# A decoder step on one Trainium2 core: split keys stored and loaded again, cached memory steps spread, sample projections on two banks

## The chip, the cores and the metric

The kernel runs on one core of a Trainium2 chip. The core has five engines with instruction streams of their own: TensorE (PE in the profile, its weight loads PEld), VectorE (DVE), ScalarE (ACT), GpSimd (POOL) and SyncE (SP, used here only to issue DMAs). Engines meet through semaphores; DMA queues are fed by SP, POOL and ACT. Operands stay in the on-chip state buffer, products go to PSUM, which has eight banks of 512 fp32 columns by 128 partitions.

The metric is the device time of one execution in microseconds. The kernel before was run three times: 1905.01, 1898.7 and 1908.0 us, median 1905.01.

## What is computed

One step of a hybrid decoder layer, for a prompt group of 1024 tokens and a sample group of 8 sequences with one token each, which share the weights (model width 1024). In the reference, cut to what matters:

```
q, k, v, logf, u, z = mixer_inputs(rmsnorm(xp, g_mix), w_in, b_f, g_sgu_v)     # prompt: 8 heads of 64
xp = xp + merge_heads(fox_prompt(q, k, v, logf), sgu_prompt(...), ..., w_o)
xp = xp + cross_attend(rmsnorm(xp, g_cross), mk, mv, w_cq, w_co)               # 256 memory rows, 4 heads of 256
xp = xp + conv_ffn(rmsnorm(xp, g_ffn), ...)                                    # 2816 gated columns

s = einsum(q, k) * 64 ** -0.5 + (cq - ck);  s[kpos > qpos] = -inf              # causal, with forget sums
o = einsum(softmax(s), v)

xs = ... the same for the sample: 8192 cached tokens through a page table,
     cross_attend with the cached keys and values of 256 memory rows per sequence
```

Everything is fp32 to the tolerance of the reference. TensorE multiplies at reduced precision per pass, so the kernel writes an operand as a high part and a remainder (`h` = rounded copy, `l` = x - h) and adds three products.

## The kernel before, in words

**Two generators.** `prompt()` yields the main work with a cost per yield. The sample's work is a second generator; the driver adds each main cost to an account and, while the account holds at least `PACE[phase]`, advances the sample by one step and subtracts it (L1793-1799). In the sample's last phase, `rest`, one step costs 2.9. Program text in that order goes through a scheduler that simulates the engines and sets the order of the instructions on each of them; `behind(e)` (L1269) makes what follows wait in that order for the latest main instruction of engine `e`.

**The prompt** goes in two halves of 512 rows: projections, attention, output projection, cross attention, feed-forward. Attention of half `hf` is `attention(hf)` (L674). It runs over four head pairs, two heads of 64 in the rows 0-63 and 64-127. For a pair:

- `load(hp)` brings q, k and v rows by three DMAs on SP (k and v of all 512 or 1024 keys).
- `setup(hp, ...)`: q rows are transposed on PE (L700) and split (L706, L707 on ACT, L720 on DVE), the forget sums come by POOL DMAs from `cq_d` and `ck_d` (L708, L717). Then, for each half `kh` of the keys, four transposes on PE (L725), a copy of each head to the high part on ACT (L729), a cast that repeats it in the rows 64-127 on POOL (L731), and the remainder by a subtraction on DVE (L736). In the first half there is one key half, in the second half two. The second half's setup of the next pair is started within the present pair.
- `scores` (L751-755): for each query block of 128 a product with the high keys and one with the low keys, per 512 columns, and the mask. In the second half a score has 640 to 1024 columns and fills a double bank; then a maximum on DVE (L760) and the exponential on ACT (L761), which frees the bank.
- `turn` transposes the exponentials (L779), ACT or DVE copy them (L786, L784), `values` multiplies them with v (L795, L804 copies the result), `back` transposes and scales (L815, L817).

**PSUM.** In the second half `BA()` and `BA2()` share two double banks in turn. A pair of `BA()` calls gets the two halves of one double bank; a score takes a whole one. Scores, q transposes and key transposes follow each other on these two.

**Buffers.** `U` is a ring of 18 buffers of 4 KB per partition, `T2` of 7 of 2 KB, `KV` of 4 of 8 KB.

**The sample** first reads its 8192 cached tokens in gathers on POOL (L1326 keys, L1385 values), multiplies and reduces keys on DVE (L1332, L1336), and multiplies values on PE (L1391). Then comes `sample_rest` (L1499): `sample_proj` for w_o and w_cq (each in two column halves, `sample_out` evacuates one), the query rows through DRAM (`q2s_d`), and the cached memory steps, eight of them, one per sequence: two broadcast loads of query rows and one load of 256 memory keys on POOL, two multiplies (L1555) and one reduce (L1556) on DVE, then a yield. Softmax, the cached memory values, w_co (L1634 and after) and the sample's feed-forward follow.

**The prompt's feed-forward** runs beside these: three products per tile (L269-271), weights split by L232 (ACT) and L233 (DVE), the convolution of a tile on DVE (L1214, L1215, L1217, L1221), which reads the PSUM bank and so frees it.

Of the kernel before, what the change touches and what calls it, by code (L numbers as in the profile page):

```python
# [18 lines left out]
P = 128  # L19
# [10 lines left out]
FF = 2816  # L30
NF = FF // P
NPAGE = 64
EPS = 1e-6
NEG = -1e30
UW = 1024
# [43 lines left out]
def build(nc, tc, ctx, a, phases=None):  # L79
# [31 lines left out]
    def U(shape, dt=F32):  # L111
        n = 1
        for s in shape[1:]:
            n *= s
        t = upool.tile([P, UW], dt, tag="u", bufs=NU, name=nm("u"))[:, :n]
        if len(shape) == 3:
            t = t.rearrange("p (a b) -> p a b", b=shape[2])
        return t
# [87 lines left out]
    sgn_d = dram.tile([T, AW], F32, tag="sgn_d", name="sgn_d")  # L206
    cq_d = dram.tile([NH, 4, T], F32, tag="cq_d", name="cq_d")
    ck_d = dram.tile([NH, 4, T], F32, tag="ck_d", name="ck_d")
    an_d = dram.tile([T, AW], F32, tag="an_d", name="an_d")
    qs_d = dram.tile([NB, AW], F32, tag="qs_d", name="qs_d")  # L210
    us_d = dram.tile([NB, AW], F32, tag="us_d", name="us_d")
# [468 lines left out]
    def attention(hf, late=None, at=3):  # L680
# [3 lines left out]
        def load(hp):  # L684
            cs = slice(hp * P, (hp + 1) * P)
            qn = T2().rearrange("p (i c) -> p i c", c=P)
            nc.sync.dma_start(qn, q_d[hf * 512 : (hf + 1) * 512, cs].rearrange("(i p) c -> p i c", p=P))
            if hf == 0:
                kvn = U([P, 2 * nk, P])
                kn, vn = kvn[:, :nk, :], kvn[:, nk:, :]  # L690
            else:
                kn, vn = U([P, nk, P]), U([P, nk, P])
            nc.sync.dma_start(kn, k_d[: nk * P, cs].rearrange("(i p) c -> p i c", p=P))
            nc.sync.dma_start(vn, v_d[: nk * P, cs].rearrange("(i p) c -> p i c", p=P))
            return qn, kn, vn

        def setup(hp, qn, kn, vn):
            tr = (MS, BB, BA)[SB]()
            for i in range(4):
                nc.tensor.transpose(tr[:, i * P : (i + 1) * P], qn[:, i, :], ident)  # L700
            qab, ka, kb = [], [], []
            for j in range(2):
                h = hp * 2 + j
                rows = slice(64 * j, 64 * j + 64)
                qq = U([P, 2, 512], F32R)
                nc.scalar.activation(qq[0:64, 0, :], tr[rows, :], AF.Copy)  # L706
                nc.scalar.activation(qq[0:64, 1, :], tr[rows, :], AF.Copy)  # L707
                nc.gpsimd.dma_start(qq[64:68, 1, :], cq_d[h, :, hf * 512 : (hf + 1) * 512])  # L708
                qab.append(qq)
                if hf == 0:  # L710
                    kab = U([P, 2, 512], F32R)
                    ka.append(kab[:, 0, :])
                    kb.append(kab[:, 1, :])
                else:
                    ka.append(U([P, nk * P], F32R))
                    kb.append(U([P, nk * P], F32R))
                nc.gpsimd.dma_start(kb[j][64:68, :], ck_d[h, :, : nk * P])  # L717
            for j, qq in enumerate(qab):
                rows = slice(64 * j, 64 * j + 64)
                nc.vector.tensor_tensor(qq[64:128, 0, :], tr[rows, :], qq[0:64, 0, :].bitcast(F32), op=ALU.subtract)  # L720
            for kh in range(hf + 1):
                yield
                tr = (MS, BB, BA)[SB]()
                for i in range(4):
                    nc.tensor.transpose(tr[:, i * P : (i + 1) * P], kn[:, kh * 4 + i, :], ident)  # L725
                s = slice(kh * 512, kh * 512 + 512)
                for j in range(2):
                    rows = slice(64 * j, 64 * j + 64)
                    nc.scalar.activation(ka[j][0:64, s], tr[rows, :], AF.Copy)  # L729
                    if KP & 1 << hf:  # L730
                        nc.gpsimd.tensor_copy(ka[j][64:128, s], ka[j][0:64, s].bitcast(F32))  # L731
                    else:
                        nc.scalar.activation(ka[j][64:128, s], tr[rows, :], AF.Copy)
                for j in range(2):
                    rows = slice(64 * j, 64 * j + 64)
                    nc.vector.tensor_tensor(kb[j][0:64, s], tr[rows, :], ka[j][0:64, s].bitcast(F32), op=ALU.subtract)  # L736
            got.append((qab, ka, kb, vn))

        def scores(qkv, ls, blk, j, ii):
# [740 lines left out]
    def sample_out(n, ps, fin):  # L1480
        t = D2()
        nc.scalar.activation(t, ps, AF.Copy)
        yield 1
        ps2 = MS()
        mmul(ps2[:8, :], selS, t, start=True, stop=True)
        fin(n, ps2[:8, :])

    def sample_proj(w, xT, fin):
        for n in range(2):
            ps = MS()  # L1490
            for kk in range(4):
                if kk % 2 == 0:
                    raw = KV().rearrange("p (k n) -> p k n", n=512)
                    nc.gpsimd.dma_start(raw, w[kk * 256 : (kk + 2) * 256, n * 512 : (n + 1) * 512].rearrange("(k p) n -> p k n", p=P))
                    yield 1
                sample_mm(ps, raw[:, (kk % 2) * 2 : (kk % 2) * 2 + 2, :], kk, xT, 512)
            yield from sample_out(n, ps, fin)

    def sample_rest(xs):  # L1499
        yield 1  # L1500
# [45 lines left out]
        for b in range(8):  # L1546
            qb = [D2(), D2()]
            for n in range(2):
                nc.gpsimd.dma_start(qb[n], q2s_d[b : b + 1, n * 512 : (n + 1) * 512].broadcast_to((P, 512)))
            kv = KV()  # L1550
            nc.gpsimd.dma_start(kv.rearrange("p (a c) -> p a c", c=D), a["cmk"][b].rearrange("(a p) c -> p a c", p=P))
            kvv = kv.rearrange("p (a c) -> p a c", c=D)
            for n in range(2):
                kn = kvv[:, :, n * 512 : (n + 1) * 512]
                nc.vector.tensor_tensor(kn, kn, qb[n].unsqueeze(1).broadcast_to((P, 2, 512)), op=ALU.mult)  # L1555
            nc.vector.tensor_reduce(sS[:, :, b, :], kv.rearrange("p (a h d) -> p a h d", a=2, h=4), axis=AX.X, op=ALU.add)  # L1556
            yield 1
        yield 1
        tr = MS()
        for mt in range(2):  # L1560
# [225 lines left out]
    for t in prompt():  # L1786
        ins = nc.cur_bb.bb.instructions
        for e in (ENG.DVE, ENG.PE):
            for i in range(len(ins) - 1, max(seen, len(ins) - 400) - 1, -1):
                if ins[i].engine == e:  # L1790
                    last[e] = ins[i]
                    break
        acc[0] += t  # L1793
        most = int(t / PACE[phase[1] or phase[0]]) + 1
        while bgs and not held[0] and most and acc[0] >= PACE[phase[1] or phase[0]]:
            most -= 1
            acc[0] -= PACE[phase[1] or phase[0]]
            if next(bgs[0], None) is None:
                bgs.pop()
        seen = len(nc.cur_bb.bb.instructions)  # L1800
    for _ in bgs.pop() if bgs else ():
        pass
# [90 lines left out]
```

## Time and profile before

| | |
|---|---|
| three runs | 1905.01, 1898.7, 1908.0 us |
| the profiled execution | 1899.86 us |
| its span | 1898.1 us |
| mean granted clock of PE | 0.979 |
| PE busy | 1817.0 us, 96% |
| DVE, ACT, POOL busy | 1394.5, 755.7, 490.6 us |
| first half's attention | about 240 to 340 us of the span |
| second half's attention | about 375 to 510 us |
| the sample's cached memory steps on DVE | about 1572 to 1632 us |

How to read the rows. A row of the timeline has the start in us, the duration, the engine, the line, the operation, out<-in by the program's names with the shape, and in brackets the idle time of the engine before it with what ended it. "xN" stands for N instructions in one row. A row of the waits says which engine and line waited for which, the total in us, how often, and the longest. A row of windows has the stretch, its length, the busy time of PE, PEld, DVE, ACT and POOL, the granted clock of PE, the DMA share and GB/s. Matmuls are pipelined: a duration includes a part in which the next is already running, so the pace is read from the distance of two starts.

### The profile page before, as it was taken

What the parts mean: (1) busy time and instruction counts of PE and PEld (TensorE: products, weight loads), DVE (VectorE), ACT (ScalarE), POOL (GpSimd) and SP (SyncE); (2) the same over time, 40 slices, a digit from 0 to 9 for tenths busy, and PEclk for the clock granted to TensorE, in tenths of its full rate; (3) what the DMA queues carried; (4) which work ended last, traced back from release to release, by engine and by line L of the source; (5) the groups of instructions that cost most, each with busy time, mean ns of one, the idle gap of its engine ahead of it and who ended that gap; (6) DMA issues with size and microseconds to landing.
All of it is one profiled execution on the core that took longest, in us unless ns stands there. A gap on an engine that the chain in (4) does not pass through costs nothing.

```text
span 1898.1 us, 24082 instructions
## 1 busy us (share of the span) xinstructions
PE 1817.0 (96%) x9255; PEld 1299.4 (68%) x9255; DVE 1394.5 (73%) x1574; ACT 755.7 (40%) x1371; POOL 490.6 (26%) x429
## 2 busy tenths in 40 slices
PE   8999999788899999999999999998999999999998
PEld 5987666555676667777767776775675667667765
DVE  4888678776678786989989998888764548754344
ACT  5332356565633534424233243325353333232332
POOL 1342242222122332313431322344222012101110
PEclk9999999989999999999999999999999999999999
DMA  8867988853397875869878879888859557666872
GB/s 320 292 246 278 324 319 292 280 168 126 136 376 251 337 274 214 310 229 353 307 266 311 309 298 348 340 337 300 308 218 356 198 200 271 226 223 255 323 275 101
DMA packets 156371, 517.06 MB, mean 272 GB/s; under 512 B 20168, under 2 KB 41928, under 8 KB 123488
## 3 DMA queue, kind: packets, MB, share of 16 engines
q0 software_dynamic: 56400, 339.04, 48.0%
q1 hardware_dynamic: 92944, 163.89, 24.8%
q10 hardware_dynamic: 6912, 12.59, 1.8%
q8 instruction: 73, 1.20, 0.2%
q14 instruction: 42, 0.34, 0.0%
HBM read 493.63 MB, written 21.84 MB: 272 GB/s over the span
## 4 chain that ended last, share of the span: by engine, by line
PE 82%; DVE 8%; ACT 4%; DMA 3%; issue 2%; POOL 0%; SPq 0%; DVEq 0%; POOLq 0%; ACTq 0%
PE ba L270 12%; PE ba L269 12%; PE ba L271 12%; PE bb L269 7%; PE bb L270 7%; PE bb L271 7%; PE dv L1391 6%; DVE kv L1332 2%; DMA kv<-cache_k,kidx 1%; PE dv L1634 1%; PE bb L795 1%; PE ba L993 1%; PE ba L994 1%; PE ba L995 1%; DVE wl L233 1%
## 5 line engine op out<-in xcount | busy, mean ns | idle before, releaser
L232 ACT ACTIVATE wh<-wr 128x1024 fp32r<-128x1024 f32 (+2 forms) x220 | 228.7, 1044 | 483.0 <-PE ba L270 154.6
L233 DVE TENSOR_TENSOR wl<-wr,wh 128x1024 fp32r<-128x1024 f32 (+2 forms) x220 | 262.6, 1200 | 155.4 <-PE ba L271 70.2
L1326 POOL DMA_INDIRECT kv<-cache_k,kidx x128 | 185.7, 1451 | 528.6 <-DVE s L1336 241.7
L1332 DVE TENSOR_TENSOR kv<-kv,d 128x2048 f32<-128x2048 f32 (+1 forms) x139 | 292.4, 2114 | 34.9 <-DMA kv<-cache_k,kidx 34.0
L1336 DVE TENSOR_REDUCE s<-kv 128x32 f32<-128x2048 f32 (+1 forms) x139 | 292.2, 2106 | 0.7
L1385 POOL DMA_INDIRECT kv<-cache_v,kidx x128 | 182.5, 1426 | 403.5 <-DVE s L1336 196.1
L269 PE MATMUL ba<-wh,u 128*128 128x512 f32 (+1 forms) x596 | 227.0, 382 | 0.0
L270 PE MATMUL ba<-wl,u 128*128 128x512 f32 (+1 forms) x596 | 226.2, 380 | 0.0
L271 PE MATMUL ba<-wh,u 128*128 128x512 f32 (+1 forms) x596 | 223.1, 379 | 0.7 <-DVE u L233 0.7
L269 PE MATMUL ba<-u,wh 128*128 128x512 f32 (+2 forms) x520 | 203.6, 392 | 1.2 <-DVE u L236 1.2
L270 PE MATMUL ba<-u,wh 128*128 128x512 f32 (+2 forms) x520 | 204.1, 393 | 0.0
L271 PE MATMUL ba<-u,wl 128*128 128x512 f32 (+2 forms) x520 | 202.9, 390 | 0.0
L1391 PE MATMUL dv<-kv,s 128*32 128x512 f32 x1024 | 138.2, 614 | 5.5 <-DMA kv<-cache_v,kidx 5.5
L269 PE MATMUL bb<-u,wh 128*128 128x512 f32 (+2 forms) x344 | 137.7, 400 | 0.0
L270 PE MATMUL bb<-u,wh 128*128 128x512 f32 (+2 forms) x344 | 136.4, 397 | 0.0
L271 PE MATMUL bb<-u,wl 128*128 128x512 f32 (+2 forms) x344 | 135.4, 395 | 0.0
L269 PEld LDWEIGHTS ba<-wh,u 128*128 128x128 f32 x596 | 112.5, 189 | 31.9 <-issue 8.0
L271 PEld LDWEIGHTS ba<-wh,u 128*128 128x128 f32 x596 | 111.8, 188 | 28.6 <-issue 6.3
L270 PEld LDWEIGHTS ba<-wl,u 128*128 128x128 f32 x596 | 112.5, 189 | 24.6 <-issue 3.8
L270 PEld LDWEIGHTS ba<-u,wh 128*128 128x128 f32 x520 | 98.7, 190 | 32.8 <-issue 12.6
L269 PEld LDWEIGHTS ba<-u,wh 128*128 128x128 f32 x520 | 98.8, 190 | 31.8 <-issue 7.1
L271 PEld LDWEIGHTS ba<-u,wl 128*128 128x128 f32 x520 | 98.6, 190 | 28.5 <-issue 9.3
(416 smaller groups left out, 3080.5 us busy)
## 6 DMA issues: line engine op xcount, KB each, us to landing
wr<-w_up SPq DMA_DIRECT2D x88, 512.0 KB
kv<-w_up POOLq DMA_DIRECT2D x22, 1024.0 KB
wr<-w_down SPq DMA_DIRECT2D x40, 512.0 KB
kv<-w_down POOLq DMA_DIRECT2D x11, 1024.0 KB
wr<-w_in SPq DMA_DIRECT2D x16, 512.0 KB
wr<-w_o SPq DMA_DIRECT2D x16, 512.0 KB
wr<-w_cq SPq DMA_DIRECT2D x16, 512.0 KB
wr<-w_co SPq DMA_DIRECT2D x16, 512.0 KB
```

Of the source, the lines that this page charges most:

```text
L232: nc.scalar.activation(h, src, AF.Copy)
L233: nc.vector.tensor_tensor(l, src, h.bitcast(F32), op=ALU.subtract)
L269: mmul(out, sh, mh, start=(i == 0), stop=False)
L270: mmul(out, sh, ml, start=False, stop=False)
L271: mmul(out, sl, mh, start=False, stop=(i == n - 1))
L795: mmul(po[64 * j : 64 * j + 64, q0:256], vn[:, kt, 64 * j : 64 * j + 64], pt[j][kt // 4][:, kt % 4, q0:256], start=(kt == 0), stop=(kt == ...
L993: mmul(pss[i], mh[k][:, tb], wh, start=(k == korder[0]), stop=False)
L1326: nc.gpsimd.indirect_dma_start(kv, None, a["cache_k"], off(kidx[:, b, ch : ch + 1]))
L1332: nc.vector.tensor_tensor(kvv[:, i : i + m, :], kvv[:, i : i + m, :], qb.unsqueeze(1).broadcast_to((P, m, 512)), op=ALU.mult)
L1336: nc.vector.tensor_reduce(s[:, ch * 4 + i : ch * 4 + i + m, :].rearrange("p k h -> p (k h)"), kvv[:, i : i + m, :].rearrange("p k (h d) -> ...
L1385: nc.gpsimd.indirect_dma_start(kv, None, a["cache_v"], off(kidx[:, b, ch : ch + 1]))
L1391: mmul(dv[32 * j : 32 * j + 32, :], s[:, ch * 4 : ch * 4 + 4, :].rearrange("p k h -> p (k h)"), kvv[:, j, :], start=(ch == 0), stop=(ch == ...
```

## The change

Three edits.

1. The first half's attention, after each setup, stores the split keys of the pair to a new DRAM tile `ks_d`: for each of the two heads the high and the low part, 64 rows of 512, on POOL's queue. The second half's setup has only its own key half to transpose and split; the first half's high part is loaded twice (rows 0-63 and 64-127) and the low part once, per head, on SP's queue. The k rows that the second half loads are those of its own half alone, into a `T2` buffer instead of a `U` buffer.
2. The cached memory steps stand behind the latest main DVE instruction, their reduce is cut into two, and each step costs three paces (`CMK`) instead of one.
3. `sample_proj` puts its two column halves into two PSUM banks (`DV`, `MS`), and both are evacuated after both products have been issued.

```diff
+CMK = 3
...
+    ks_d = dram.tile([NH, 64, 2, 512], F32, tag="ks_d", name="ks_d")
...
-                kn, vn = U([P, nk, P]), U([P, nk, P])
-            nc.sync.dma_start(kn, k_d[: nk * P, cs].rearrange("(i p) c -> p i c", p=P))
+                kn, vn = T2().rearrange("p (i c) -> p i c", c=P), U([P, nk, P])
+            nc.sync.dma_start(kn, k_d[hf * 512 : nk * P, cs].rearrange("(i p) c -> p i c", p=P))
...
                     ka.append(U([P, nk * P], F32R))
                     kb.append(U([P, nk * P], F32R))
+                    for r in range(2):
+                        nc.sync.dma_start(ka[j][64 * r : 64 * r + 64, 0:512].bitcast(F32), ks_d[h, :, 0, :])
+                    nc.sync.dma_start(kb[j][0:64, 0:512].bitcast(F32), ks_d[h, :, 1, :])
...
-            for kh in range(hf + 1):
+            for kh in (hf,):
                 yield
                 tr = (MS, BB, BA)[SB]()
                 for i in range(4):
-                    nc.tensor.transpose(tr[:, i * P : (i + 1) * P], kn[:, kh * 4 + i, :], ident)
+                    nc.tensor.transpose(tr[:, i * P : (i + 1) * P], kn[:, i, :], ident)
...
+            if hf == 0:
+                for j in range(2):
+                    nc.gpsimd.dma_start(ks_d[hp * 2 + j, :, 0, :], ka[j][0:64, :].bitcast(F32))
+                    nc.gpsimd.dma_start(ks_d[hp * 2 + j, :, 1, :], kb[j][0:64, :].bitcast(F32))
...
-        ps2 = MS()
+        ps2 = (DV, MS)[n]()
...
     def sample_proj(w, xT, fin):
+        outs = []
         for n in range(2):
-            ps = MS()
+            ps = (DV, MS)[n]()
...
-            yield from sample_out(n, ps, fin)
+            outs.append(sample_out(n, ps, fin))
+            next(outs[n])
+        for o in outs:
+            yield from o
+        yield 1
...
-            for n in range(2):
-                kn = kvv[:, :, n * 512 : (n + 1) * 512]
-                nc.vector.tensor_tensor(kn, kn, qb[n].unsqueeze(1).broadcast_to((P, 2, 512)), op=ALU.mult)
-            nc.vector.tensor_reduce(sS[:, :, b, :], kv.rearrange("p (a h d) -> p a h d", a=2, h=4), axis=AX.X, op=ALU.add)
-            yield 1
+            with behind(ENG.DVE):
+                for n in range(2):
+                    kn = kvv[:, :, n * 512 : (n + 1) * 512]
+                    nc.vector.tensor_tensor(kn, kn, qb[n].unsqueeze(1).broadcast_to((P, 2, 512)), op=ALU.mult)
+                for i in range(2):
+                    nc.vector.tensor_reduce(sS[:, i, b, :], kvv[:, i, :].rearrange("p (h d) -> p h d", h=4), axis=AX.X, op=ALU.add)
+            yield CMK
...
-            if next(bgs[0], None) is None:
+            w = next(bgs[0], None)
+            if w is None:
                 bgs.pop()
+            else:
+                acc[0] -= (w - 1) * PACE[phase[1] or phase[0]]
```

The line numbers shift by 2 to 16: L725 becomes L730, L736 L741, L751 L760, L760 L769, L779 L788, L817 L826, L1326 L1335, L1332 L1341, L1336 L1345, L1385 L1394, L1555 L1570, L1556 L1572. The stores are L744 and L745.

The order of instructions moves in three places. The first is PE within the second half's attention, in the setup for the third head pair, before (`ba` are the double banks, `u_3736` the k rows):

```order
L725 MATMUL ba_3878<-cp,u_3736 128x128 x4
...
L751 MATMUL ba_3891<-u_3546,u_3542 128x512
...
L755 MATMUL ba_3891<-cmask_b,ident_b 128x128
L725 MATMUL ba_3927<-cp,u_3736 128x128 x4
L751 MATMUL ba_3940<-u_3553,u_3549 128x448
...
L779 MATMUL bb_3965<-cp,wr_3889 128x128 x4
L779 MATMUL bb_3971<-cp,wr_3889 128x128 x4
L751 MATMUL ba_3957<-u_3553,u_3549 128x512
```

and now (`t_748_3743` holds the k rows of the second half alone):

```order
L730 MATMUL ba_3891<-cp,t_748_3743 128x128 x4
...
L760 MATMUL ba_3904<-u_3558,u_3554 128x512
...
L764 MATMUL ba_3904<-cmask_b,ident_b 128x128
L760 MATMUL ba_3942<-u_3568,u_3564 128x448
...
L760 MATMUL ba_3959<-u_3568,u_3564 128x512
...
L788 MATMUL bb_3967<-cp,wr_3902 128x128 x4
L788 MATMUL bb_3973<-cp,wr_3902 128x128 x4
```

The second group of transposes is gone from between the two scores, and the third score has moved ahead of the transposes of exponentials.

The second place is DVE in the setup before that, for the second head pair; before:

```order
L736 TENSOR_TENSOR u_3554<-ba_3581,u_3553 64x512
L1332 TENSOR_TENSOR kv_3592<-kv_3592,d_388_2404 128x1024 x2
L760 TENSOR_REDUCE mx_3609<-ba_3610 128x1
L1336 TENSOR_REDUCE s_2406<-kv_3592 128x16
L817 TENSOR_TENSOR u_3669<-bb_3671,rl_3633 128x128 x2
L1336 TENSOR_REDUCE s_2406<-kv_3592 128x16
L736 TENSOR_TENSOR u_3547<-ba_3646,u_3546 64x512
L736 TENSOR_TENSOR u_3554<-ba_3646,u_3553 64x512
L760 TENSOR_REDUCE mx_3658<-ba_3659 128x1
```

and now:

```order
L741 TENSOR_TENSOR u_3569<-ba_3599,u_3568 64x512
L1341 TENSOR_TENSOR kv_3610<-kv_3610,d_388_2409 128x1024 x2
L769 TENSOR_REDUCE mx_3627<-ba_3628 128x1
L1345 TENSOR_REDUCE s_2411<-kv_3610 128x16
L826 TENSOR_TENSOR u_3676<-bb_3678,rl_3651 128x128 x2
L769 TENSOR_REDUCE mx_3665<-ba_3666 128x1
L1345 TENSOR_REDUCE s_2411<-kv_3610 128x16
```

One pair of subtractions is gone, and the maximum of the 896-wide score stands ahead of the second reduce of the sample (`s_2411`).

The third place is POOL's queue in the first half's attention, at the third pair's setup, as it is now:

```order
L722 DMA u_2754<-ck_d 4x512
L744 DMA ks_d<-u_2748 64x512
L744 DMA ks_d<-u_2754 64x512
L1335 DMA kv_3177<-cache_k,kidx 128x2048
L745 DMA ks_d<-u_2748 64x512
L745 DMA ks_d<-u_2754 64x512
L1394 DMA kv_3194<-cache_v,kidx 128x2048
```

Before, the two gathers (L1326, L1385) stood there without the stores. In the first pair all four stores stand together ahead of a gather of keys.

On DVE, the first multiply of the memory steps stands behind the second up-projection tile of the third group of the second half's feed-forward, where it stood behind the fifth.

## The prediction

> **What bounds the kernel now.** I read the page first: the engines' totals and the chain of work that ended last.
>
> ```profile
> PE 1817.0 (96%) x9255; PEld 1299.4 (68%) x9255; DVE 1394.5 (73%) x1574; ACT 755.7 (40%) x1371; POOL 490.6 (26%) x429
> PE 82%; DVE 8%; ACT 4%; DMA 3%; issue 2%; POOL 0%; SPq 0%; DVEq 0%; POOLq 0%; ACTq 0%
> ```
>
> TensorE is the bound. Time can be won only where PE idles or runs at a lower granted clock. So I went to the stretches that the change touches: the second half's attention (about 375 to 510 us of the span) and the sample's cached memory steps (about 1570 to 1635 us). The first two rows below are 50 us stretches, the others 10 us. The columns are the length, the busy time of PE, PEld, DVE, ACT and POOL (with instructions), the granted clock, the DMA share and GB/s.
>
> ```profile
> 400.00:450.00 50.00, 38.96 (x238) 27.30 (x237) 33.11 (x48) 28.40 (x56) 14.27 (x17) 0.84 0.46 152
> 450.00:500.00 50.00, 43.48 (x277) 31.21 (x276) 31.02 (x41) 26.59 (x54) 8.45 (x12) 0.88 0.40 138
> 420.00:430.00 10.00, 9.52 (x45) 7.18 (x46) 4.90 (x7) 5.38 (x11) 0.00 (x0) 0.62 0.44 167
> 450.00:460.00 10.00, 9.00 (x46) 6.97 (x46) 6.52 (x8) 5.04 (x10) 0.00 (x0) 0.76 0.33 105
> 480.00:490.00 10.00, 7.47 (x31) 6.03 (x30) 7.01 (x10) 4.96 (x9) 1.22 (x2) 0.66 0.27 80
> 1550.00:1560.00 10.00, 10.00 (x41) 6.96 (x39) 4.86 (x7) 3.91 (x6) 0.00 (x0) 1.00 0.64 256
> 1560.00:1570.00 10.00, 10.00 (x49) 6.15 (x49) 6.24 (x10) 3.31 (x7) 2.00 (x3) 1.00 0.82 277
> 1610.00:1620.00 10.00, 3.62 (x10) 2.66 (x9) 10.00 (x12) 2.23 (x3) 0.71 (x1) 0.77 0.74 260
> ```
>
> PE idles 17.6 us of these 100 us of attention, and in the sample's steps it loses 6.4 us at once while DVE is full. The waits of PE in each place (columns: total us, times, longest):
>
> ```profile
> PE ba L751 <- ACT wr L761: 9.0, 5, 3.0
> PE bb L269 <- DVE t L1217: 6.4, 1, 6.4
> ```
>
> **Keys: where the wait comes from.** Scores (L751) and the transposes of the setup (L725) alternate between two double banks. In the setup of the last head pair, with a clock drop behind it:
>
> ```profile
> 477.10 0.40 PE L751 MATMUL ba<-u,u 128*128 128x512 f32 x1
> 477.34 0.39 PE L753 MATMUL ba<-u,u 68*128 68x512 f32 x1
> 479.40 0.63 PE L725 MATMUL ba<-cp,u 128*128 128x128 f32 x4 [0.83 <-DVE u L736]
> 482.56 0.74 PE L751 MATMUL ba<-u,u 128*128 128x448 f32 x1 [2.53 <-ACT wr L761]
> 485.91 0.78 PE L751 MATMUL ba<-u,u 128*128 128x512 f32 x1
> 486.91 0.63 PE L751 MATMUL ba<-u,u 128*128 128x512 f32 x1
> 487.34 0.63 PE L753 MATMUL ba<-u,u 68*128 68x512 f32 x1
> 489.13 0.39 PE L751 MATMUL ba<-u,u 128*128 128x320 f32 x1
> ```
>
> ```profile
> 477.85 1.41 DVE L736 TENSOR_TENSOR u<-ba,u 64x512 fp32r<-64x512 f32 x2 [3.71 <-ACT u L729]
> 479.29 1.23 DVE L760 TENSOR_REDUCE mx<-ba 128x1 f32<-128x1024 f32 x1
> 481.31 1.39 DVE L736 TENSOR_TENSOR u<-ba,u 64x512 fp32r<-64x512 f32 x2 [0.40 <-ACT u L729]
> 480.07 1.21 ACT L729 ACTIVATE u<-ba 64x512 fp32r<-64x512 f32 x2 [0.97 <-PE ba L725]
> 481.30 1.11 ACT L761 ACTIVATE wr<-ba,mx 128x1024 f32<-128x1024 f32 x1
> ```
>
> The second set of key transposes (479.40) takes the bank that the first L736 frees at 479.26. So the 896-wide score needs the other bank, which the 1024-wide score holds until its exponential ends at 482.41. In the new order only one set is left, in the place of the first, and the 896-wide score follows the 1024-wide one. It then needs the bank that L736 frees at 479.26: it starts 3.3 us earlier (482.56 - 479.26). What is late next is the following 1024-wide score. It needs the exponential of the first one. That one no longer stands behind the two copies of 1.21 us on ACT: the maximum ends at 480.52, the exponential at about 481.6, and the score starts there instead of at 485.91: **4.3 us**. Head pairs 2 and 1, in the same way:
>
> ```profile
> 445.97 1.23 DVE L760 TENSOR_REDUCE mx<-ba 128x1 f32<-128x1024 f32 x1
> 452.59 0.78 PE L751 MATMUL ba<-u,u 128*128 128x512 f32 x1
> 411.04 2.35 DVE L1332 TENSOR_TENSOR kv<-kv,d 128x1024 f32<-128x1024 f32 x2
> 414.55 1.21 DVE L1336 TENSOR_REDUCE s<-kv 128x16 f32<-128x1024 f32 x1
> 418.61 1.09 DVE L760 TENSOR_REDUCE mx<-ba 128x1 f32<-128x896 f32 x1
> ```
>
> Pair 2: the maximum ends at 447.20 and the exponential of 1.11 us at 448.3, so the score at 452.59 moves by 4.2 us. Pair 1 is slowed by DVE: the sample's L1332 runs ahead of the maximum, so the first exponential stays where it is, and the next two scores hang on DVE. The 896-wide maximum (418.61) loses one pair of L736, 1.39 us, and one L1336 of 1.21 us from ahead of it in the new order, so it can win 2.6; I take **2.5**. Together 4.3 + 4.2 + 2.5 = 11.0 us. Pair 0 has all four copies of ACT in one row, and its setup stands ahead of the first score:
>
> ```profile
> 376.09 2.44 ACT L729 ACTIVATE u<-ba 64x512 fp32r<-64x512 f32 x4
> ```
>
> Half of it goes: 1.2 us. The bounds of these two are 0 (another wait fills the gaps) and 12.2.
>
> The clock: matmuls of 512 columns follow each other at 0.43 us (486.91 and 487.34) where they did at 0.24 (477.10 and 477.34). By the granted clock the three 10 us rows above lose 3.8, 2.4 and 3.4 us, 9.6 together. About 3.0 of that lies before the scores at 452.59 and 485.91 and is counted already. Of the 6.6 left I take a third, 2.2, since an idle of about 1.3 us remains in each pair, from the end of the earlier 896-wide score to the exponential at 481.6; bounds 0 and 6.6. The Trainium skill ("TensorE: Matmul & The Clock Gate", Part 1: The HAM clock gate) says that the array falls to half rate after an idle window of about 3.4 us and needs about 3.4 us of work to return, in free-running windows. The trace agrees in kind (0.62 to 0.76 behind idles of 2.5 to 3.0 us); by that rule the idles that are left would trip nothing, all 6.6 us would come back, and the whole sum below would be 22.4 instead of 18.0.
>
> **Keys: what it costs.** Sixteen stores of 128 KB from POOL's queue, 24 loads of 128 KB on SP's, less 1 MB of keys that is not loaded again. POOL's issues and waits from 230 to 345 us:
>
> ```profile
> L717 POOL DMA_DIRECT2D u<-ck_d x7 | 3.8, 549 | 0.7 <-ACT t L758 0.7
> POOL kv L1385 <- DVE s L1336: 24.5, 3, 13.7
> POOL kv L1326 <- DVE s L1336: 18.8, 4, 7.4
> ```
>
> Sixteen issues at 0.55 us are 8.8 us, less than the 43 us in which POOL waits there for DVE. Eight casts of keys leave POOL. The loads of a pair stand about 15 us ahead of its scores on SP and have the buffers that the pair before frees, so I cost them at nothing; were they late, the pair's first score would wait. Two places may pay. Towards 300 us the DMA engines are full (share 1.02):
>
> ```profile
> 290.00:300.00 10.00, 10.00 (x54) 6.99 (x47) 8.48 (x10) 5.86 (x12) 4.89 (x6) 0.95 1.02 382
> ```
>
> About 1 MB of stores lands around there: 2.7 us at the row's 382 GB/s, if a load that PE awaits is behind it, else 0. And the last pair's stores precede POOL's load of the query sums for the second half:
>
> ```profile
> 373.90 0.59 ACT L706 ACTIVATE u<-ba 64x512 fp32r<-64x512 f32 x1 [3.75 <-DMA u<-cq_d]
> ```
>
> That load is waited for; two to four issues ahead of it are 1.1 to 2.2 us. I take 2.4 for both, about half of the upper end of 4.9; the lower is 0. Keys: 11.0 + 1.2 + 2.2 - 2.4 = **12.0 us**.
>
> **Memory steps.** DVE has 16 multiplies (L1555) and 8 reduces (L1556) there, and waits for the query rows ahead of the first:
>
> ```profile
> 1572.16 1.23 DVE L1555 TENSOR_TENSOR kv<-kv,d 128x1024 f32<-128x1024 f32 x1 [2.16 <-DMA d<-q2s_d]
> 1580.01 2.28 DVE L1556 TENSOR_REDUCE sS<-kv 128x8 f32<-128x2048 f32 x1
> 1616.70 0.77 PE L269 MATMUL bb<-wh,u 128*128 128x512 f32 x1 [6.38 <-DVE t L1217]
> 1621.96 0.53 PE L270 MATMUL ba<-wl,u 128*128 128x512 f32 x1
> ```
>
> DVE is full, and its backlog stops PE at 1610.3 for 6.38 us and halves the clock until about 1622.3: 5.6 us are 13 matmuls at 0.43, and at 0.24 they would take 2.5 less. So at most 8.9 us are to be won. In the new order the first L1555 stands three up-projection tiles earlier: 72 matmuls of 0.24, 17 us. In the 20 us from 1550 DVE idles 5.1 + 3.8 = 8.9 us, so in 17 us some 7 us of the work fit in. The split reduces cost 8 x (2 x 1.21 - 2.28) = 1.1 more, with 1.21 from L1336, which reads as many elements. Seven less 1.1 nearly covers 6.38. I take **6.0** with bounds 0 and 8.9; the wait for the query rows, 2.16 us, moves ahead with the first L1555. Two banks for the projections: PE is busy 10.00 of 10 us in both rows from 1550, where they run, so nothing.
>
> **The sum.** 12.0 + 6.0 = 18.0 us. The profiled execution took 1899.9 us around a span of 1898.1; so it would be 1881.9, and the median of the three runs, 5.2 above that execution, goes from 1905.0 to **1887**.
>
> **The rivals.**
> 1. Only one part pays: the memory steps still end before the same split of the up phase in the new order, so DVE's backlog may stand as before (keys alone: 1893), or the keys' gaps are refilled by DVE in front of the maxima, as L1332 does in pair 1 (steps alone: 1899). For it: DVE is full from 1610 to 1620. Against: DVE idles 17 and 19 of the 50 us in attention. About 1896.
> 2. No change: both gaps move elsewhere. The next wait after the 896-wide score is again an exponential, which speaks for it; the chain above against it. About 1903.
> 3. Slower: a store of a low key half stands on POOL until DVE's subtraction (L736) is done, ahead of the cache gathers. If that hold is longer than POOL's slack, the sample's attention and the cq_d load are late. The waits above show gathers stuck for 7.4 and 13.7 us. At 7.4 us in each of four pairs, less the forecast's gain, it is 1905 + 4 x 7.4 - 18 = 1917. It decides once a store holds POOL longer than the 7.4 us that a gather waits for DVE anyway. Against it: DVE's pair of subtractions takes 1.4 us.
> 4. More than forecast: the whole 6.6 us of clock and the 8.9 of the burst come back, and no store costs: 12.2 + 6.6 + 8.9 = 27.7, so 1877.
>
> The Trainium skill ("SBUF — State Buffer", SBUF: two separate sides) speaks against stores from POOL: descriptors of a GpSimd DMA starve while DVE holds the shared port. The trace does not show that for plain copies (549 ns each, with DVE busy 8.48 of 10 us); by the rule rival 3 would be likelier.
>
> **How the numbers follow.** Forecast 0.46, one part 0.20, no change 0.13, slower 0.12, more 0.09. A measurement of this kernel tells 0.5%, 9.5 us, from no change: faster means under 1895.5. The forecast and rival 4 lie there, and about half of rival 1: 0.66. Rivals 2, the rest of 1 and a few hundredths of 3 are the same: 0.24. Slower: 0.10. The range goes from 1876 (rival 4) to 1906 (all costs at their upper ends against a part of the gain); the forecast's own is 1880 to 1894.
>
> **What would show it.** In the profile after: no 2.5 to 3.0 us wait of the 896-wide score for an exponential, the third score of each pair starting at the end of the first one's exponential, and a clock over 0.9 in the three 10 us stretches. In the steps: no 6.4 us wait for L1217, DVE busier just ahead of them. Wrong would be: PE waiting for the loads of stored keys, POOL's stores standing for DVE with gathers late behind them, or the DVE backlog with its stall at a later up tile.

## The result and the profile after

Ten runs of the changed kernel took 1882.67 to 1891.37 us, median **1889.12 us**; ten of the kernel before took 1895.84 to 1909.6 us, median 1904.68. The ratio is 0.9919 with a 95% interval of 0.9902 to 0.9936: faster by 0.8%, some 15 us. The forecast was 1887 us.

From the page of the kernel after, the engines' totals and the chain:

```profile
PE 1809.0 (96%) x9239; PEld 1295.5 (69%) x9239; DVE 1388.9 (74%) x1574; ACT 750.9 (40%) x1363; POOL 484.1 (26%) x437
PE 82%; DVE 6%; DMA 6%; ACT 4%; issue 2%; POOL 0%; SPq 0%; DVEq 0%; POOLq 0%; ACTq 0%
```

TensorE is still the bound; its busy time fell by 8 us and DVE's share of the chain from 8% to 6%. The stretches of the prediction, each at its new place (in the same columns as before):

```profile
400.00:450.00 50.00, 40.84 (x264) 29.96 (x264) 35.37 (x51) 29.85 (x62) 12.38 (x14) 0.90 0.61 185
450.00:500.00 50.00, 46.51 (x310) 32.37 (x312) 30.96 (x45) 30.06 (x63) 7.21 (x10) 0.93 0.44 143
440.00:450.00 10.00, 7.83 (x35) 6.56 (x35) 6.85 (x9) 4.94 (x10) 0.00 (x0) 0.66 0.36 125
470.00:480.00 10.00, 7.86 (x35) 6.33 (x33) 7.31 (x10) 5.57 (x10) 0.38 (x1) 0.67 0.44 115
1610.00:1620.00 10.00, 9.93 (x44) 7.66 (x43) 10.00 (x13) 3.37 (x4) 0.72 (x1) 1.00 0.61 199
```

PE idles 12.7 us of the 100 us of attention where it idled 17.6, and the hole of 6.4 us in the memory steps is gone (9.93 of 10 us busy, full clock), with DVE still full. The work of the steps now lies ahead of it: DVE is busy 9.78 and 10.00 us in the two rows from 1550 us, where it was 4.86 and 6.24 before.

```profile
1550.00:1560.00 10.00, 10.00 (x45) 8.15 (x44) 9.78 (x11) 3.88 (x6) 2.19 (x5) 1.00 0.82 259
1560.00:1570.00 10.00, 10.00 (x45) 8.12 (x44) 10.00 (x12) 3.12 (x7) 2.47 (x4) 1.00 0.80 272
```

But the clock in the setups of the last two pairs, at 440 and 470 us, is 0.66 and 0.67, where it was 0.76 and 0.66. The last pair's setup, on PE and then on DVE and ACT, answers to the rows at 477 to 489 us of before:

```profile
468.43 0.48 PE L760 MATMUL ba<-u,u 128*128 128x512 f32 x1
471.35 0.44 PE L760 MATMUL ba<-u,u 128*128 128x448 f32 x1 [0.89 <-DVE u L741]
473.75 0.79 PE L760 MATMUL ba<-u,u 128*128 128x512 f32 x1 [1.26 <-ACT wr L770]
474.76 0.63 PE L760 MATMUL ba<-u,u 128*128 128x512 f32 x1
475.19 0.63 PE L762 MATMUL ba<-u,u 68*128 68x512 f32 x1
```

```profile
469.79 1.41 DVE L741 TENSOR_TENSOR u<-ba,u 64x512 fp32r<-64x512 f32 x2 [3.76 <-POOL u L736]
471.23 1.23 DVE L769 TENSOR_REDUCE mx<-ba 128x1 f32<-128x1024 f32 x1
472.49 1.11 ACT L770 ACTIVATE wr<-ba,mx 128x1024 f32<-128x1024 f32 x1 [1.50 <-DVE mx L769]
```

The 896-wide score waits for the only subtraction that is left, which frees its bank, and the 1024-wide one behind it for the first exponential, as the prediction had it: the second is the wait that it called "late next". Their idles of 0.89 and 1.26 us stand where idles of 0.83 and 2.53 us stood, and the matmuls behind them again take 0.63 us. In all, the waits of scores for exponentials fell from 9.0 us to 5.9, the longest in pair 1:

```profile
PE ba L760 <- ACT wr L770: 5.9, 4, 2.6
```

**Where the time went.** I paired the matmuls that both traces have, line by line and in their order, and took the difference of their starts, after less before, in us:

```
at (us of before)   250   345   385   410   419   444   453   477   486
after - before      +0.8  +2.0  +0.7  -1.1  -4.1  -5.2  -9.3  -8.1  -12.2
at (us of before)   515   550   600   700   1100  1475  1580  1650
after - before      -10.3 -11.2 -6.8  -6.9  -6.2  -2.6  -3.3  -13.4
```

(410 to 486 are, two by two, the first 1024-wide score beside a setup and the score behind the 896-wide one, in the setups for pairs 1 to 3.) Four things are to be seen. By 345 us, where the stores stand, 1.2 us are lost; but in the profiles of `e2_steps_banks` and `e5_bank` below, which have no stores, 1.9 and 2.5 us are lost there, so these 1.2 can't be put down to the stores. The second attention wins: from +0.8 to -10.3, 11.1 us net. Then 4.3 us are **given back** between 575 and 600 us, in code that the change does not touch. And from 1580 to 1650 us the memory steps win 10.1 us. The slow loss between 1100 and 1475 us lies in code that the change leaves alone: the trace of before has 13.7 us of half clock from 1100 to 1480 us and that of after 23.9, and the later experiments lie between 10.2 and 23.9. The rows of the page's waits in that give-back are, before (566 to 614 us) and after (555 to 605 us):

```profile
PE ba L1027 <- DVE u L236: 2.2, 1, 2.2
PE ba L1043 <- DVE u L236: 1.9, 1, 1.9
```

```profile
PE ba L607 <- issue: 2.2, 1, 2.2
PE bb L271 <- DVE u L238: 2.2, 1, 2.2
PE ba L1036 <- DVE u L961: 2.1, 1, 2.1
PE bb L272 <- DVE u L238: 1.7, 1, 1.7
```

8.2 us of waits instead of 4.1. The instructions of DVE stand in another order there: work of the spatial gate (L589, L599) and a multiply of the sample (L1341) now run ahead of all the last column pieces of the normalised rows (L238, 128x128), where before one to three of these pieces ran first, and PE waits for the pieces. That the scheduler placed them so because it came there in another state is argued, not shown.

### The profile page after: what moved, and what is told of

It is laid out like the page before. It is cut to its first block, busy times and chain, and to the rows that moved or that the text cites. A ratio compares the mean times of both kernels' runs of the same rounds, so it can differ in the third digit from the quotient of the medians.

```text
span 1885.8 us, 24147 instructions
## 1 busy us (share of the span) xinstructions
PE 1809.0 (96%) x9239; PEld 1295.5 (69%) x9239; DVE 1388.9 (74%) x1574; ACT 750.9 (40%) x1363; POOL 484.1 (26%) x437
## 4 chain that ended last, share of the span: by engine, by line
PE 82%; DVE 6%; DMA 6%; ACT 4%; issue 2%; POOL 0%; SPq 0%; DVEq 0%; POOLq 0%; ACTq 0%
PE ba L271 12%; PE ba L273 12%; PE ba L272 12%; PE bb L271 7%; PE bb L272 6%; PE bb L273 6%; PE dv L1400 6%; DMA kv<-cache_k,kidx 2%; DVE kv L1341 1%; DVE s L1345 1%; PE dv L1650 1%; PE ba L1002 1%; PE ba L1004 1%; PE ba L1003 1%; DMA wr<-w_ck 1%
## 5 line engine op out<-in xcount | busy, mean ns | idle before, releaser
L1341 DVE TENSOR_TENSOR kv<-kv,d 128x2048 f32<-128x2048 f32 (+1 forms) x139 | 292.6, 2114 | 30.2 <-DMA kv<-cache_k,kidx 30.1
L1335 POOL DMA_INDIRECT kv<-cache_k,kidx x128 | 174.1, 1360 | 529.1 <-DVE s L1345 251.0
L1345 DVE TENSOR_REDUCE s<-kv 128x32 f32<-128x2048 f32 (+1 forms) x139 | 292.1, 2106 | 0.6
L1394 POOL DMA_INDIRECT kv<-cache_v,kidx x128 | 181.1, 1415 | 420.8 <-DVE s L1345 196.6
L272 PEld LDWEIGHTS ba<-u,wh 128*128 128x128 f32 x520 | 99.4, 191 | 34.4 <-issue 11.1
```

The lines of the kernel that those rows point to most:

```text
L272: mmul(out, sh, ml, start=False, stop=False)
L1335: nc.gpsimd.indirect_dma_start(kv, None, a["cache_k"], off(kidx[:, b, ch : ch + 1]))
L1341: nc.vector.tensor_tensor(kvv[:, i : i + m, :], kvv[:, i : i + m, :], qb.unsqueeze(1).broadcast_to((P, m, 512)), op=ALU.mult)
L1345: nc.vector.tensor_reduce(s[:, ch * 4 + i : ch * 4 + i + m, :].rearrange("p k h -> p (k h)"), kvv[:, i : i + m, :].rearrange("p k (h d) -> ...
L1394: nc.gpsimd.indirect_dma_start(kv, None, a["cache_v"], off(kidx[:, b, ch : ch + 1]))
```

## The experiments

All ratios are to runs of the kernel before on the same chip, with a 95% interval; us are medians.

### Each edit alone, and the two of the sample together

`e1_keys` has the diff's hunks on `ks_d`, `load` and `setup` alone; `e2_steps_banks` those on `sample_proj`, `sample_out`, the memory steps and the account; `e3_steps` the memory steps and the account alone; `e4_banks` `sample_proj` and `sample_out` alone.

> The keys' edit alone (stores, loads, one transposed key half); memory steps and projections as before. Theory (the two edits add up, the keys win where the 896-wide score waited): the second attention ends some 11 us earlier than before against its start, part is given back in the set-up of the second half's cross attention (4.3 us in the profile after, at about 575 to 597 us), the 6.4 us wait for the convolution stays; time 5 to 10 us below before. Rival (the give-back takes all, the change is worth only its memory steps): within 3 us of before.

Measured: 1898.78 us, ratio 0.9972 (0.9960 to 0.9985), 5.6 us below before. The second attention won as in the change (11.0 us in the paired starts from 385 to 515 us, in both), the give-back at 570 to 600 us was 6.5, and the stall in the memory steps was 8.3 us in this profile:

```profile
PE bb L270 <- DVE t L1225: 8.3, 1, 8.3
```

> The memory steps and the two banks, keys as before. Theory: the 6.4 us wait and the 6.8 us of half clock behind it are gone, 9 to 10.8 us below before. Rival (half of the gain of the memory steps hangs on the keys' earlier end or is chance): 3 to 5 us below.

Measured: 1894.24 us, ratio 0.9950 (0.9930 to 0.9970), 10.2 us below before. The wait is gone, as the theory had it. 5.6 and 10.2 are 15.8, the whole is 15.6: **the keys and the sample's edits add up**, within intervals of about 2.4 and 3.8 us on the two parts.

> The memory steps alone: behind the latest main DVE instruction, reduce in two, three paces a step; one PSUM bank for the projections as before. The first multiply then stands where it stood before, three weight splits later than in the change. Theory A (what helps is that the steps begin earlier): little is won, 0 to 4 us below before, a wait for the convolution stays. Theory B (what helps is that the steps are spread by their paces): 7 to 10 us below before and no such wait.

Measured: 1902.45 us, ratio 0.9995 (0.9976 to 1.0013): nothing that can be told. The wait stays nearly whole:

```profile
PE bb L270 <- DVE t L1218: 6.1, 1, 6.1
PE ba L271 <- DVE wl L234: 1.4, 1, 1.4
```

> The two banks alone; memory steps at one pace each, reduce whole. The first multiply stands three weight splits earlier on DVE than before and the last two earlier. Theory A (the earlier start helps): 6 to 10 us below before, the wait under 2 us. Theory B (the spreading helps): the steps are as dense as before, so a wait of about 6 us stays at an earlier up tile, within 3 us of before.

Measured: 1901.92 us, ratio 0.9999 (0.9982 to 1.0016): nothing either. So theory A of this run fell: an earlier start alone is not worth 6 to 10 us. Theory B had the time right, but its wait of 6 us is not there; there are two shorter ones, one of them new:

```profile
PE ms L1566 <- DVE sS L1561: 2.1, 1, 2.1
PE bb L269 <- DVE t L1215: 1.4, 1, 1.4
1610.00:1620.00 10.00, 6.29 (x22) 4.01 (x21) 10.00 (x14) 4.56 (x9) 1.43 (x2) 0.87 0.75 251
1620.00:1630.00 10.00, 10.00 (x36) 7.98 (x35) 8.56 (x18) 5.72 (x9) 0.00 (x0) 0.79 0.43 159
```

With the steps dense and early, PE waits in its order for the last reduce (the sample's transposes stand ahead of the main products), then for the convolution, and loses the clock over both. Neither edit of the sample is worth anything by itself, both are worth 10 us.

### Which part of the memory steps does it

`e7_pace1` is the change with `CMK = 1`; `e10_cmk5` with `CMK = 5`; `e11_nobehind` leaves out the tie to the main DVE work:

```diff
-            with behind(ENG.DVE):
+            with nullcontext():
```

> The whole change with CMK = 1: the memory steps start as early as in the change, are behind the latest main DVE instruction and have the reduce in two, but come as densely as before. Theory A (early start and the three paces are both needed): a wait of 2 to 6 us for the convolution is back, with half clock behind it, 3 to 8 us above the change. Theory B (the order behind the main DVE work does it, the paces nothing): no such wait, within 2 us of the change.

Measured: 1900.91 us, ratio 0.9978 (0.9964 to 0.9992), 11.8 us above the change; more than theory A's 3 to 8. The waits are small, but there are several, and the clock falls behind them:

```profile
PE ms L1577 <- DVE sS L1572: 1.8, 2, 0.9
PE bb L271 <- DVE t L1224: 1.5, 1, 1.5
1610.00:1620.00 10.00, 6.30 (x17) 4.47 (x18) 10.00 (x16) 4.17 (x8) 0.71 (x1) 0.70 0.92 326
```

> The whole change without the tie to the latest main DVE instruction; three paces, split reduces and two banks stay. In the order the steps are then as dense as with one pace. Theory (the tie is what lets the paces act): a wait for the convolution and half clock are back, 8 to 14 us above the change, like the kernel with one pace. Rival (the paces suffice): within 3 us of the change.

Measured: 1897.97 us, ratio 0.9967 (0.9953 to 0.9981), 8.9 us above the change: the tie is needed, as expected. In the paired starts of this profile the main products go from -3.9 us at 1580 to between -4.6 and -6.5 from 1645 to 1680 us, where the change has -13.4 throughout. Half clock did not come back in it, against the theory's words, only waits.

> The whole change with five paces a memory step: the last step lies behind the 192nd weight split instead of the 188th, and in the order no main matmul is left behind the sample's last ones. Theory (the steps have enough room at three, and the sample's tail becomes the end): no wait for the convolution, 3 to 12 us above the change, with the sample's work alone at the end. Rival (more room helps DVE further): within 2 us of the change or below.

Measured: 1894.14 us, ratio 0.9934 (0.9916 to 0.9953); the median is 5.0 us above the change, though the intervals of the two overlap. No wait for the convolution is left, but the span ends in the sample's work, with PE idle for 3.6 and 2.3 of 10 us and the DMA engines near full:

```profile
1863.00:1873.00 10.00, 6.39 (x34) 2.65 (x33) 3.93 (x8) 1.09 (x4) 3.29 (x5) 1.00 1.01 393
1873.00:1883.00 10.00, 7.73 (x26) 1.47 (x28) 0.00 (x0) 0.00 (x0) 0.00 (x0) 0.83 0.86 339
PE dv L1689 <- DMA kv<-w_down: 5.9, 4, 2.2
```

So the gain has three conditions, each shown by a run that lacks it: an early start (banks), the tie, and more than one pace a step. A fourth, not so many paces that the tail becomes the end, is seen in the profile of `e10_cmk5` but not clear of noise in its times.

### The keys: the bank or the work?

`e5_bank` is the kernel before with one line changed, and `e8_bank_steps` the same line on top of the sample's edits, in place of all stores and loads:

```diff
-                tr = (MS, BB, BA)[SB]()
+                tr = BB() if kh == 1 else (MS, BB, BA)[SB]()
```

> The kernel before with one line changed: the transposes of the second key half go to a bank of their own kind (bb) instead of a double bank. All work of the setup stays (transposes, copies, casts, subtractions, no store or load); the 896-wide score then finds the bank that the first subtractions free. Theory A (the wait was for the bank): the 896-wide score no longer waits 2.5 to 3.0 us for the exponential of the 1024-wide one, the attention shortens by 4 to 9 us of the 11 that the keys' edit won there, time 3 to 9 us below before. Theory B (what helps is the work that the keys' edit takes from ACT and DVE): the waits only change their name, within 2 us of before.

Measured: 1895.63 us, ratio 0.9965 (0.9952 to 0.9978), 7.8 us below before. All copies, casts and subtractions are still there. The waits of scores for exponentials in the second attention were 9.0 us with a longest of 3.0; here are their sum, and the 896-wide score and the 1024-wide one behind it in pair 1. The first no longer waits:

```profile
PE ba L751 <- ACT wr L761: 4.7, 5, 2.1
415.63 0.45 PE L751 MATMUL ba<-u,u 128*128 128x448 f32 x1
419.08 0.50 PE L751 MATMUL ba<-u,u 128*128 128x512 f32 x1 [2.08 <-ACT wr L761]
```

> The memory steps and the two banks of the change, with the one line of the separate key bank in place of the stored keys. Theory A (the wait was for the bank): within 4 us of the change without any store or load. Theory B (work removed): 4 to 6 us above the change.

Measured: 1889.07 us, ratio 0.9931 (0.9918 to 0.9944): the change's 1889.12 to within its uncertainty. The wait was for the **bank**. The half of the setup's work that the keys' edit takes from PE, ACT, DVE and POOL adds nothing that can be measured, and with it falls the need for the 16 stores and 24 loads. The give-back is there too: in the profile of `e5_bank` the same four waits behind the attention take 2.2, 2.2, 2.1 and 1.5 us. So it doesn't come from stores or loads. It shows in each of the profiles in which the second attention is shortened by the keys' edit or the bank (4.1 to 6.7 us are lost from 575 to 600 us), and in none of the other four (0.7 us at most). `e2_steps_banks`, one of these, loses 4.9 us from 600 to 700 us instead, so losses of this size are not bound to an early end.

`e6_stores` adds the sixteen stores to the kernel before, and nothing reads them.

> The kernel before with the sixteen stores on POOL's queue and nothing that reads them. Theory (the stores lie in POOL's waits): 0 to 3 us above before. Rival (gathers and the load of the query sums are held up behind a store that stands for DVE): 6 us or more above before, the start of the second attention late by as much.

Measured: 1901.84 us, ratio 0.9989 (0.9975 to 1.0002): no cost. On POOL of the changed kernel, from 230 to 375 us (busy us, mean ns | idle before, by releaser):

```profile
L744 POOL DMA_DIRECT2D ks_d<-u x8 | 4.4, 552 | 16.2 <-ACT u L734 16.0 <-issue 0.2
L745 POOL DMA_DIRECT2D ks_d<-u x8 | 4.3, 543 | 4.5 <-DMA u<-ck_d 3.0 <-DVE u L741 1.3 <-issue 0.2
```

The low parts held POOL 1.3 us in all for DVE's subtraction, and the high parts 16 us for ACT's copy. As the time doesn't grow with them, the rival of stores that hold up the gathers is out. In the profile of the change no wait of PE is put down to a load of `ks_d` either.

### More banks, and the clock

`e9_both_banks` moves the changed kernel's one set of key transposes to `bb` as well, so that scores alone share the double banks:

```diff
-                tr = (MS, BB, BA)[SB]()
+                tr = BB() if hf else (MS, BB, BA)[SB]()
```

> The whole change, and the one set of key transposes that is left in the second attention goes to bb, so that scores alone use the two double banks. Theory (the exponentials of the scores set the pace once the setup has no bank): the five or so waits of scores for exponentials shrink from 5.9 to about 4 us, 0 to 4 us below the change. Rival (the setup's transposes wait for bb, which the transposes of exponentials use): 2 to 6 us above the change.

Measured: 1886.71 us, ratio 0.9884 (0.9860 to 0.9908). The median is 2.4 us below the change, but the intervals of the ratios overlap. The waits for exponentials did not shrink, against the theory's words:

```profile
PE ba L760 <- ACT wr L770: 7.4, 5, 2.5
```

The last experiment asked why the clock stayed at 0.66. The clock records of the traces hold only two values, 1.0 and 0.5, in stretches whose lengths are multiples of 3.413 us on a fixed grid. I took each 3.413 us of that grid in the thirteen traces at hand (from the first half-clock stretch on), the share of it in which PE was busy with matmuls, and the clock of the next one:

```
PE busy share of 3.413 us   under 40%   40-50%     50-60%     60% and more
full clock: half follows    98 of 98    66 of 86   15 of 55   1 of 5641
PE busy share               under 70%   70-80%     80-90%     90% and more
half clock: half stays      45 of 45    22 of 24   15 of 32   11 of 172
```

In the change, PE was busy for 54% and 48% of the stretch ahead of the half clock of pairs 2 and 3 (0.89 and 1.26 us of idle, with the five matmuls of one score between, in pair 3). `e12_filler` therefore adds products that nobody reads ahead of the 896-wide score of the second head, to the changed kernel:

```diff
                         drain(LA[hf])
+                        if hf and hp < 3 and (blk, j, ii) == (1, 1, 0):
+                            fill = BB()
+                            for _ in range(6):
+                                mmul(fill[:, :512], qkv[0][j][:, 0, 0:P], qkv[1][j][:, 0:512], start=True, stop=True)
                         yield 1.8
```

> The whole change with six added products of 128x512 into a free bb bank ahead of the 896-wide score of the second head, in the three pairs with a setup; nobody reads them. They take 6 x 0.24 = 1.4 us of PE where it stands idle for 0.9 and 1.3 us in the profile after (2.6 in the pair of 410 us). Over all traces so far a stretch of 3.41 us with PE under 40% busy was followed by half clock each time, and one with over 60% by full clock each time but one. Theory (the half clock in these pairs comes from the idle shares, and costs time): the half-clock stretches at about 415, 443 and 473 us (17 us in all) are gone or shorter, 3 to 8 us below the change. Rival 1 (scores hang on the exponentials there, so PE at full clock only waits longer): the stretches go, but the time stays within 2 us. Rival 2 (the added products delay the scores): 3 to 6 us above the change.

Measured: **1879.91 us** (four runs, 1878.43 to 1882.12), ratio 0.9873 (0.9852 to 0.9895): 9.2 us below the change (8.8 by the two ratios), 1.3% below before. The setup for pair 2, the third, and the 10 us stretches from 410, 440 and 470 us:

```profile
437.72 1.65 PE L876 MATMUL bb<-u,u 128*128 128x512 f32 x6
439.21 0.36 PE L760 MATMUL ba<-u,u 128*128 128x448 f32 x1
441.15 0.50 PE L760 MATMUL ba<-u,u 128*128 128x512 f32 x1 [0.88 <-ACT wr L770]
441.49 0.40 PE L762 MATMUL ba<-u,u 68*128 68x512 f32 x1
410.00:420.00 10.00, 7.81 (x50) 6.01 (x48) 8.97 (x12) 6.73 (x14) 4.05 (x4) 1.00 0.87 313
440.00:450.00 10.00, 8.90 (x63) 6.45 (x62) 8.44 (x10) 7.13 (x14) 0.00 (x0) 1.00 0.14 41
470.00:480.00 10.00, 9.71 (x74) 7.38 (x75) 9.70 (x12) 6.02 (x14) 1.03 (x1) 1.00 0.16 54
```

The clock records of half clock between 340 and 520 us (start, length in us):

```
before   366.1 6.8   379.7 3.4   403.6 3.4   417.3 10.2   448.0 6.8   482.1 6.8
after    364.2 3.4   377.8 6.8   415.4 3.4   442.7 6.8    473.4 6.8
filler   363.1 3.4   376.7 6.8
```

The three stretches of 17 us are gone, and the paired starts against the change go from -1.0 at 400 us to -7.0 at 520 us: 6.0 us won there, where half of 17 us, 8.5, is the most that half clock can have cost. The two profiled spans are 9.2 us apart (1885.8 and 1876.6); the other 3.2 us lie ahead of 400 us (1.0) and behind 520 us (2.2), where nothing was changed, so some 6 us are shown to be won in this place. From 400 to 520 us of the change PE was busy for 107.1 us and idle for 12.9; in the same work with the filler (399 to 513 us) it was busy for 104.6 and idle for 9.4. The 18 added products are in the 104.6, 4.5 us at their distance of 0.25. So the rest of the work took 7.0 us less, near the 8.5 that half clock can have cost: that part is the clock's. The idle fell by 3.5, for the 4.5 put in. Rival 1 (only longer waits) and rival 2 (scores delayed) are out. One thing is untested: the added line also takes a bank of the `bb` rotation, and some fifty of PE's instructions stand in another order, so the fall of the idle need not be all the filler's; no run takes the bank without the products.

## Why the prediction was right, and where it was not

**The total** was 18 us against a measured 15.6, 1887 against 1889: right within its own range. Its parts were less so: the keys alone brought 5.6 us where 12.0 were forecast, the sample's edits 10.2 where 6.0 were. Two errors of opposite sign cancelled, and that the total came so close is in good part luck.

**The keys' places** were right. Forecast were 2.5, 4.2 and 4.3 us for pairs 1 to 3, from the score behind the 896-wide one. In the paired starts it is 3.0 (from 1.1 to 4.1 us ahead), 4.1 (5.2 to 9.3) and 4.1 (8.1 to 12.2). Pair 0's setup won 1.3 with 1.2 forecast. For the stores and the loads ahead of the second half 2.4 were forecast; `e6_stores` shows no cost of the stores. The wait that took the place of the old one is the one that the prediction named. `e5_bank` shows that the bank is the cause.

**The clock term** failed in the step "of the 6.6 left I take a third". Outside the places above the pairs won 2.9 us and lost 3.0, so in time nothing of it came. Pairs 2 and 3 kept their 6.8 us of half clock each; pair 1's fell from 10.2 to 3.4, and the matmuls behind its place won 1.1 us at most with that. Nor is the fall over the whole attention clear of chance. Between 400 and 520 us the trace of before has 27.3 us of half clock, but `e2_steps_banks`, `e3_steps` and `e4_banks`, with the same code there, have 20.5 and `e6_stores` 13.7; the change, `e1_keys`, `e7_pace1` and `e11_nobehind` have 17.1. (The separate bank does better: 6.8 in `e5_bank`, 10.2 in `e8_bank_steps`.) The step saw the idle of about 1.3 us that stays (1.26 measured), but not the 0.89 just ahead of it, and the two together are enough. Its 6.6 was too large as well, since it reckons the lower clock over the whole 10 us of each row, and PE idled for 0.5, 1.0 and 2.5 us of them. The rule of the Trainium skill ("TensorE: Matmul & The Clock Gate", Part 1: The HAM clock gate), by which all 6.6 us would have come back, is right here in the two values and in the length of the window; in the word "idle" the traces differ. A stretch that is less than 40% busy halved the clock each time (98 of 98), an empty one or not, and the measurement decides. `e12_filler` shows that half clock costs time in this place: 7.0 us of PE's work went with 17 us of it, once the idle was filled.

**What the keys' sum left out** is the give-back of 4.3 us behind the attention (6.5 in the profile of `e1_keys`). The step that failed is the unsaid one that time won at 500 us arrives at the end. Together with the clock term it is why the keys alone brought 5.6 us, not 12.0.

**The memory steps** were mis-sized in the other direction: 6.0 forecast, 10.2 measured (5.7 to 13.3 by the interval), and 10.1 in the paired starts, above the upper bound of 8.9. That bound held the stall of 6.38 and 2.5 of clock, and left out a wait for a weight split in the same place:

```profile
PE ba L271 <- DVE u L233: 0.7, 1, 0.7
```

With it the terms come to 9.6 of the 10.1 us. The lower value came from the step that let only 7 us of work fit in ahead. What it left out is that the tie and the paces also keep the main work ahead in DVE's order: DVE is full (10.00 of 10 us) and PE doesn't wait, and without either of the two (`e11_nobehind`, `e7_pace1`) waits are back.

**Two banks** were costed at nothing because PE is busy there. That was the wrong question. The edit moves no work of PE, but it lets the first multiply start earlier, and the prediction had that move in its sum without saying which edit made it. Alone it is worth nothing (`e4_banks`), without it the spread is worth nothing (`e3_steps`).

**The rivals.** One part alone: refuted by `e1_keys` and `e2_steps_banks`, both pay. No change: refuted by the interval of the ratio. Slower through POOL: refuted by `e6_stores`. More than forecast: the burst did come back whole, the clock in the attention did not.

**Left open:** why the order behind the attention comes out worse in every profile in which it ends earlier through the keys' edit or the bank, and whether another setting of the scheduler takes the 4 us back. That was not tried. Nor is `e9_both_banks` told apart from the change.

## What to carry to other kernels

Before moving work away from an engine, ask whether the wait is for the work or for the buffer: one line that sends a set of transposes to other banks (`e8_bank_steps`) did what 40 DMAs and half a setup less did. On the engine that bounds the kernel, count what idle is left in each few microseconds rather than the longest idle; where dependences leave idle that can't be closed, products that nobody reads may pay for themselves through the clock. And spreading a burst on a shared engine takes an earlier start and a tie to the main work together; test such edits in pairs before dropping one as useless.

## What the runs showed of the hardware

The granted clock has two values and a grid of 3.413 us. It fell mostly when PE was busy for less than half of one stretch, always below 40%, sometimes from 50 to 60% (15 of 55), and once in 5641 at 60% or more. At half clock it came back mostly from 80% on and never below 70% (0 of 45). So two idles of 0.89 and 1.26 us close together cost as much half clock (6.8 us, pair 3 of after) as idles of 0.83 and 2.53 did (6.8 us, pair 3 of before). That it depends on where an idle falls in the grid follows from the table, but no run here moves one. Between 1100 and 1480 us, in code that no edit touches, the traces hold 10.2 to 23.9 us of half clock, so two single executions can differ by several us there, and medians of several runs have to be compared.
